# Three edits to the order of work at a seam: end transposes behind three of four contraction tiles, one split exchanged, and a group of transposes moved by one step

## The chip, the cores and the metric

The kernel runs on one core of one Trainium2 chip. The metric is the device time in microseconds (us) of one execution. Engines are named as the profile names them: PE is TensorE's matmuls, PEld its weight loads, DVE is VectorE, ACT is ScalarE, POOL is GpSimd, SP is SyncE.

## The reference

The model is a two-layer decoder trunk over 512 tokens of width 1024: a gated short-convolution layer with its feed-forward part, then a sliding-window attention layer (16 heads of 64, 4 key/value heads, window 128, a sink per head) with its feed-forward part. Cut to what lies on both sides of the seam:

```python
# end of layer 0
ff = swiglu(rmsnorm(h, ffn_pre_norm[0]), ffn_w_gate_up[0], ffn_w_down[0])
h = h + rmsnorm(ff, ffn_post_norm[0])
# start of layer 1
kv = rmsnorm(h, kv_norm) @ w_kv                 # shared keys and values
q = (rmsnorm(h, b_pre_norm[0]) @ b_w_q[0])      # queries
```

Both normed inputs of layer 1 have the same row factor and differ in the gain of each feature alone: one gain for keys and values (`kv_norm`), one for queries (`b_pre_norm`).

## The kernel before, in words

Everything is fp32, and products keep nearly fp32's accuracy with three matmuls in a short format: each operand is split into a rounded part `hi` (made by ACT) and a remainder `lo` (made by DVE, which reads `hi`), and `mm3` issues `whi*xlo`, `whi*xhi`, `wlo*xhi`.

The residual stream `h` lies as four tiles of 128 tokens by 1024 features (t = 0 to 3). What follows needs it with the features on the partitions, so the class `Update` does, for each token tile t: add the new contribution (`take`), sum its squares (`square_mix`), scale by the gain behind the norm (`scale`), work out the row factor (`mean`, DVE, with a power on POOL), update `h` (`update`), sum the squares of the new `h` (`square`), the next row factor (`mean2`, DVE and POOL), and scale into `xn[t]` (`norm`, ACT). Then `turn(b, ts)` transposes on PE the feature tiles b and b+4 of the token tiles `ts` into one PSUM bank, and `split(n, f, hf)` reads a quarter of such a bank for feature tile f twice: ACT writes `hi` (L350), DVE writes `lo` (L351). n = 0 is the copy for keys and values, n = 1 that for queries. hf = 0 holds the tokens of t = 0 and 1, hf = 1 those of t = 2 and 3. So a bank b of one half is read by four splits, each by two engines: (0, b), (0, b+4), (1, b), (1, b+4). There are two banks in each of two pools for these tiles, so that bank b of half 1 is the bank b of half 0 over again.

The seam runs so:

- `close` (L869) ends the feed-forward part: eight units of PE work (token tile t, half of the output columns), each with `n` = 4 contraction tiles of three matmuls of 512 columns. In the last unit, t = 3, half 1, the transposes of the tokens 0 and 1 (16, four per bank) stand between contraction tiles, and behind the unit the four splits (0, 0..3) of half 0 are issued. `close` is called three times (L961, L1188, L1534); the second call is this seam.
- `last_tile` (L909) then holds the norm of the last two token tiles and, in the gaps, lists of splits of half 0, called `pieces`. `pieces[3]` stands ahead of `norm(3)`, `pieces[4]` behind it.
- The loop at L1431 makes keys and values on PE: for each half, for each feature tile k, 12 matmuls of 256 columns. In half 0, behind k = 6 and k = 7, stand the transposes of the tokens 2 and 3 (`turn(b, (2, 3))`) with the splits (0, b) of half 1. Half 1 of the loop reads those.

The whole runs in the program's own order on PE, DVE, ACT and POOL (`tc.manual_schedule(engines=ALL)`): each engine works through its instructions in the order in which these lines issue them, and the framework adds the waits. Loads go through SP's queue and sums of weight blocks in memory through POOL's.

Of the kernel before, what the change touches and what calls it, by code (L numbers as in the profile page):

```python
# [73 lines left out]
def yoco_kernel(  # L74
# [38 lines left out]
    def name(s):  # L113
        uid[0] += 1
        return f"{s}_{uid[0]}"
# [13 lines left out]
    def bank(s, pool=None):  # L129

        if pool is None:
            pool = (ps_mm, ps_sc, ps_mm, ps_pt)[turn[0] % 4]
            turn[0] += 1
        return pool.tile([P, S], F32, tag="bank", name=name(s))
# [39 lines left out]
    def split_weights(src, raw=None, slots=False):  # L174
        if raw is None:
            raw = fetch(src)
        if slots:
            hi, lo = Two("whi", F32R), Two("wlo", F32R)
            for h in range(2):
                c = slice(h * S, (h + 1) * S)  # L180
                nc.scalar.activation(hi[:, c], raw[:, c], AF.Copy)
                nc.vector.tensor_tensor(out=lo[:, c], in0=raw[:, c], in1=hi[:, c].bitcast(F32),
                                        op=ALU.subtract)
            return hi, lo
        hi = wsp.tile([P, D], F32R, tag="whi", name=name("whi"))
        lo = wsp.tile([P, D], F32R, tag="wlo", name=name("wlo"))
        nc.scalar.activation(hi, raw, AF.Copy)
        nc.vector.tensor_tensor(out=lo, in0=raw, in1=hi.bitcast(F32), op=ALU.subtract)
        return hi, lo
# [14 lines left out]
    def unit(ps, t, ws, x, ks, n, k0=0, c0=0, c1=S):  # L204

        tk = slice(t * P, (t + 1) * P)
        for k in ks:
            w = ws[k // 2]
            kk = slice((k % 2) * S + c0, (k % 2) * S + c1)
            mm3(ps, x[k0 + k][0][:, tk], x[k0 + k][1][:, tk], w[0][:, kk], w[1][:, kk],  # L210
                k == 0, k == n - 1)
# [344 lines left out]
    for l in range(2):  # L556
# [3 lines left out]
        for rd, (f0, f1) in enumerate(ROUNDS[:-1]):  # L560
            k = slice(f0 // 2, f1 // 2)
# [50 lines left out]
    def seven(acts, n, mix, first):  # L612
# [9 lines left out]
        def product(p, ks, hi, lo):  # L622
# [34 lines left out]
    ws = [[wsp.tile([P, D], F32R, tag=tag, name=name(tag)) for tag in ("whi", "wlo")]  # L657
          for _ in range(3)]
# [10 lines left out]
    with tc.manual_schedule(engines=ALL):  # L669
# [25 lines left out]
        for k in range(KT):  # L695
# [7 lines left out]
            for i in range(3):  # L703
                for t in range(3):
                    n = 3 * k + t
# [9 lines left out]
        ws = [split_weights(None, raw, True) for raw in later[:2]]  # L715
# [21 lines left out]
    ys, acts, mix_c = [], [], [None] * NB  # L737
    both = []
    res = Update(mix_c, B_CONV, [G_FPRE[0]])
# [83 lines left out]
    with tc.manual_schedule(engines=ALL):  # L823
# [29 lines left out]
        ws = [line[f"w{n}"].w for n in range(4)]  # L853
# [12 lines left out]
        if square:  # L866
            res.square(t)

    def close(ws, x, k0, res, ahead, then=None, each=2):  # L869


        n = len(x) - k0

        def part(ps, t, half, ks):
            unit(ps, t, ws[len(ws) // 2 * half :], x, ks, n, k0)

        begun = [bank("pmix", ps_mm) for _ in range(2)]
        for half in range(2):
            part(begun[half], 0, half, range(n - 1))
            for _ in range(each if half == 0 or each > 1 else 0):  # L880
                ahead.one()
        for t in range(NB):
            for half in range(2):
                if t == 0:
                    ps = begun[half]
                    part(ps, t, half, range(n - 1, n))
                else:
                    ps = bank("pmix", ps_mm)
                    if (t, half) == (NB - 1, 1):
                        part(ps, t, half, range(2))  # L890
                        for b in range(4):
                            res.turn(b, (0, 1))
                        part(ps, t, half, range(2, n))
                        for f in range(4):
                            res.split(0, f, 0)
                        res.square_mix(t, 0)
                        res.square(NB - 2)
                        res.scale(t, 0)
                    else:
                        part(ps, t, half, range(n))  # L900
                res.take(t, half, ps)
                if (t, half) != (NB - 1, 0):
                    res.square_mix(t, half)
            if t < NB - 1:
                tile_done(res, t, square=t < NB - 2)
            if t == 0 and then:
                then()

    def last_tile(res, pieces, ahead=None):  # L909


        def some(i):
            for n, *f in pieces[i]:
                if n == "keep":
                    res.keep(f[0], 0, f[1])
                elif n == "weights":
                    ahead.slots()
                else:
                    res.split(n, f[0], 0)

        res.mean2(2)
        res.norm(2)
        res.mean(3)
        res.scale(3, 1)
        some(0)
        res.update(3)
        some(1)
        res.square(3)
        some(2)
        res.mean2(3)  # L930
        some(3)
        res.norm(3)
        some(4)
# [14 lines left out]
    def first_weights(l):  # L948
        return ([w_gu[l, f, j] for f in range(2) for j in range(2)]
                + [w_gb[l, 0, b] for b in range(2)])  # L950
# [3 lines left out]
    ahead = Ahead(first_weights(0))  # L954
# [9 lines left out]
    def ffn(l, before, ahead, gain, gpres, following):  # L964
# [152 lines left out]
        acts = [[] for _ in ROUNDS]  # L1117
        mix = [None] * NB
        pss = [bank("pgu", ps_mm) for _ in range(4)]
        with tc.manual_schedule(engines=ALL):  # L1120
# [44 lines left out]
            n = f1 - f0  # L1165
# [12 lines left out]
        res = Update(mix, gain, gpres)  # L1178
# [5 lines left out]
        ws = [job.w for job in closing]  # L1184
        if gpres:
            ahead = Ahead(following)
            with tc.manual_schedule(engines=ALL):
                close(ws, acts[-1], 0, res, ahead)  # L1188
            return res, ahead
        with tc.manual_schedule(engines=ALL):  # L1190
            for t in range(NB):
                for half in range(2):
                    if (t, half) == (NB - 1, 1):
                        for c in (0, 256):
                            ps = bank("pmix")
# [5 lines left out]
                    else:  # L1201
                        ps = bank("pmix")
# [16 lines left out]
    res, ahead = ffn(0, res, ahead, B_FFN[0], [G_KV, G_BPRE], [  # L1219
        w_k[0], w_k[1], w_v[:, 0:D], w_v[:, D:], w_q[0], w_q[1]])  # L1220
# [205 lines left out]
    at = []  # L1426

    with tc.manual_schedule(engines=ALL):
        last_tile(res, [[(0, 4)], [(0, 5)], [], [(0, 6), (0, 7), (1, 0), (1, 1)],
                        [(1, f) for f in (4, 5, 2, 3, 6, 7)]])  # L1430
        for hf in range(2):  # L1431
            c = slice(hf * 256, (hf + 1) * 256)
            for k in range(KT):
                kk = slice(k * P, (k + 1) * P)
                for ps, (whi, wlo) in zip(pk, wk):
                    mm3(ps[:, c], whi[:, kk], wlo[:, kk], xkv[k][0][:, c], xkv[k][1][:, c],
                        k == 0, k == KT - 1)
                values(2 * hf, k)
                values(2 * hf + 1, k)
                if hf == 0 and k >= 6:  # L1440
                    for b in (2 * k - 12, 2 * k - 11):
                        res.turn(b, (2, 3))
                        res.split(0, b, 1)
            if hf == 0:
                for f in range(4, KT):
                    res.split(0, f, 1)
            if hf == 0:
                ahead.one()
                for f in range(KT):
                    res.split(1, f, 1)  # L1450
                ahead.one()
                qs[0].w, qs[1].w = ahead.ready[4:]


        vt = [halves("vt", F32R) for _ in range(NB)]
        for pair in vt:
            for v in pair:
                nc.gpsimd.memset(v.bitcast(F32), 0.0)

        last_p = [slot("lp", F32R) for i in range(2)]  # L1460
        for p in last_p:
            nc.gpsimd.memset(p.bitcast(F32), 0.0)
        for part in range(4):
            qs[0].project(part)
        ks = [rope_split(rope(pk[0], nc.vector), nc.vector)]
        qs[LEAD].weights()
        nc.scalar.activation(warm, ones[:, 0:1], AF.Exp)
        for part in range(4):
            qs[1].project(part)
        qs[0].rotate(nc.vector)  # L1470
        qs[0].split(nc.vector)
        dst = [[v.rearrange("p (h d) -> p h d", d=2 * HD)[:, :, :HD] for v in pair]
               for pair in vt]
        src = [p.rearrange("p (h d) -> p h d", d=HD) for p in pv]
        for j in range(NB):
            nc.scalar.activation(dst[j][0], src[j], AF.Copy)
        for j in range(NB):
            nc.vector.tensor_tensor(out=dst[j][1], in0=src[j], in1=dst[j][0].bitcast(F32),
                                    op=ALU.subtract)

    with tc.manual_schedule(engines=ALL):
        sum_on("a0")
        for i in range(KT + 2):
            if i == KT:
                res = Update(mix_o, B_ATT, [G_FPRE[1]])
                res.leaves = True
                ahead = Ahead(first_weights(1))
            if i == KT + 1:
                res.load()
            for c in ORDER.split():  # L1490
# [13 lines left out]
                op, n = c[0], [int(d) for d in c[1:].rstrip("-")]  # L1504
                t = i - late
# [19 lines left out]
                else:  # L1525
                    t = 2 * (t - EARLY - 1) + n.pop(0)
# [104 lines left out]
```

## Time and profile before

| | before |
|---|---|
| median of 3 runs | 1020.13 us (1019.88 to 1020.14) |
| profiled execution, its own time | 1020.08 us |
| its span | 1018.3 us |
| PE / PEld / DVE / ACT / POOL busy | 99% / 88% / 85% / 57% / 19% |
| mean granted clock of TensorE | 0.999 |
| the seam (first of the end transposes to the first matmul of half 1) | 508.83 to 525.99 us of the span |

A row of the timeline gives the start of a group of instructions in us of the span, the time from its first start to its last end, the engine, the line, the tiles written and read, how many there are, and in brackets the engine's idle time before them with what ended it. Matmuls overlap: what counts for PE is the distance from start to start. The row of a line's own view gives the shortest, median and longest duration in ns. The waits view gives the engine, what waited, what it waited for, and the sum, number and longest of the waits in us.

### The profile page before, as it was taken

Reading aid. Unit: us, or ns where it says so; the run is one execution under the profiler, and the core shown is the slowest. Engines: PE = TensorE matmul, PEld = TensorE weight load, DVE = VectorE, ACT = ScalarE, POOL = GpSimd, SP = SyncE. Lnnn points to the kernel's source line nnn. Section 1 sums busy time; section 2 is a strip of 40 time slices with the busy share of each in tenths; the row PEclk is TensorE's granted clock in tenths of the full one; section 3 lists DMA queues with packets and bytes.
Section 4 is the critical chain, followed back from the end, with each engine's and each line's share of the span. In section 5 each row is a group of like instructions: output and inputs, shape, how many; then the busy total and the mean of one; then the engine's idle time right before and its main releaser. Section 6 shows DMA issues by size and latency. Waiting matters only on the chain.

```text
span 1018.3 us, 16274 instructions
## 1 busy us (share of the span) xinstructions
PE 1009.6 (99%) x6008; PEld 892.7 (88%) x6008; DVE 867.5 (85%) x1480; ACT 581.2 (57%) x1035; POOL 194.6 (19%) x259
## 2 busy tenths in 40 slices
PE   9999999999999999999999999999999999999997
PEld 8888888999889898998898888889998998989986
DVE  5766767899789999998869998778997899999896
ACT  6322444875655555566566776677666564645641
POOL 0443033102101011000122653221111010110001
PEclk9999999999999999999999999999999999999999
DMA  9997789549979699779504889976899576979742
GB/s 355 288 269 220 183 257 344 158 166 279 343 239 297 216 298 334 234 219 324 183 2 141 205 243 273 246 278 151 270 291 330 169 245 233 284 273 273 245 164 83
DMA packets 66575, 244.50 MB, mean 240 GB/s; under 512 B 7872, under 2 KB 8384, under 8 KB 54720
## 3 DMA queue, kind: packets, MB, share of 16 engines
q1 hardware_dynamic: 51328, 145.98, 38.8%
q0 software_dynamic: 14592, 96.48, 37.5%
q8 instruction: 47, 0.77, 0.3%
q10 hardware_dynamic: 576, 1.02, 0.3%
q14 instruction: 32, 0.26, 0.1%
HBM read 237.15 MB, written 102.76 MB: 334 GB/s over the span
## 4 chain that ended last, share of the span: by engine, by line
PE 93%; DVE 3%; ACT 2%; issue 1%; DMA 0%; POOL 0%; DVEq 0%; SPq 0%; ACTq 0%
PE gx L1055 14%; PE gx L1058 7%; PE pcub L194 4%; PE pcub L192 4%; PE pcub L193 4%; PE gz L194 4%; PE gz L193 4%; PE gz L192 4%; PE px L192 3%; PE px L193 3%; PE px L194 3%; PE pmix L193 2%; PE pmix L192 2%; PE pmix L194 2%; PE gy L194 2%; PE gy L193 2%
## 5 line engine op out<-in xcount | busy, mean ns | idle before, releaser
L478 DVE TENSOR_TENSOR wlo<-raw,whi 128x1024 fp32r<-128x1024 f32 x225 | 274.6, 1225 | 53.1 <-ACT whi L477 53.0
L477 ACT ACTIVATE whi<-raw 128x1024 fp32r<-128x1024 f32 x225 | 233.6, 1050 | 102.3 <-DVE raw L465 28.7
L1055 PE MATMUL gx<-xt,whi 128*128 128x512 f32 x480 | 120.4, 393 | 0.0
L1055 PEld LDWEIGHTS gx<-xt,whi 128*128 128x128 f32 x480 | 86.3, 189 | 15.5
L546 POOL DMA_DIRECT2D hsum<-in_w_gb_dram x96 | 62.8, 735 | 151.0 <-ACT whi L477 90.2
L546 POOL DMA_DIRECT2D hsum<-hsum x32 | 25.2, 789 | 294.3 <-ACT whi L477 219.3
L1017 DVE TENSOR_TENSOR st<-gx,st 128x256 f32<-128x256 f32 x200 | 77.9, 419 | 2.6 <-ACT st L1033 0.5
L1033 ACT ACTIVATE st<-gx 128x256 f32<-128x256 f32 x120 | 43.2, 380 | 62.6 <-PE gx L1058 58.9
L1058 PEld LDWEIGHTS gx<-xt,wlo 128*128 128x128 f32 x480 | 65.5, 190 | 4.7
L1058 PE MATMUL gx<-xt,wlo 128*128 128x256 f32 x480 | 66.9, 282 | 0.0
L1069 ACT ACTIVATE gr<-gr 128x1024 f32<-128x1024 f32 x20 | 21.3, 1063 | 50.1 <-DVE gr L1017 50.1
L192 PE MATMUL px<-wlo,ahi 128*128 128x512 f32 x120 | 46.8, 390 | 0.1
L194 PE MATMUL px<-whi,alo 128*128 128x512 f32 x120 | 46.7, 389 | 0.0
L193 PE MATMUL px<-whi,ahi 128*128 128x512 f32 x120 | 46.7, 389 | 0.0
L194 PE MATMUL gz<-xhi,wlo 128*128 128x256 f32 x160 | 45.5, 284 | 0.0
L193 PE MATMUL gz<-xt,whi 128*128 128x256 f32 x160 | 45.3, 283 | 0.0
L192 PE MATMUL gz<-xt,whi 128*128 128x256 f32 x160 | 45.3, 283 | 0.0
L193 PE MATMUL gy<-xhi,whi 128*128 128x256 f32 x160 | 45.3, 283 | 0.0
L192 PE MATMUL gy<-xlo,whi 128*128 128x256 f32 x160 | 45.3, 283 | 0.0
L194 PE MATMUL gy<-xhi,wlo 128*128 128x256 f32 x160 | 45.3, 283 | 0.0
L192 PE MATMUL gz<-xlo,whi 128*128 128x256 f32 x160 | 45.3, 283 | 0.0
L194 PE MATMUL gz<-xt,wlo 128*128 128x256 f32 x160 | 45.3, 283 | 0.0
(298 smaller groups left out, 2991.7 us busy)
## 6 DMA issues: line engine op xcount, KB each, us to landing
hsum<-in_w_gb_dram POOLq DMA_DIRECT2D x96, 512.0 KB, 7.9
raw<-hsum SPq DMA_DIRECT2D x88, 512.0 KB, 8.1
raw<-in_w_gb_dram SPq DMA_DIRECT2D x60, 512.0 KB, 7.1
hsum<-in_w_dn_dram POOLq DMA_DIRECT2D x36, 512.0 KB, 8.4
raw<-in_w_dn_dram SPq DMA_DIRECT2D x32, 512.0 KB, 6.3
hsum<-hsum POOLq DMA_DIRECT2D x28, 512.0 KB, 5.6
raw<-in_w_in_dram SPq DMA_DIRECT2D x21, 512.0 KB, 7.8
hsum<-in_w_dn_dram POOLq DMA_DIRECT2D x12, 768.0 KB, 13.1
```

What stands on the lines that cost most here:

```text
L192: nc.tensor.matmul(out, whi, xlo, start=start, stop=False, **kw)
L193: nc.tensor.matmul(out, whi, xhi, start=False, stop=False, **kw)
L194: nc.tensor.matmul(out, wlo, xhi, start=False, stop=stop, **kw)
L477: self.begun = nc.scalar.activation(hi[:, :n], raw, AF.Copy)
L478: nc.vector.tensor_tensor(out=lo[:, :n], in0=raw, in1=hi[:, :n].bitcast(F32), op=ALU.subtract)
L546: nc.gpsimd.dma_start(dst, src, max_dma_last_dim=4 * 4 * S, **kw))
L1017: nc.vector.tensor_tensor(out=out, in0=a, in1=b, op=ALU.add)
L1033: nc.scalar.activation(ste, a, AF.Copy)
L1055: nc.tensor.matmul(banks[c][e], whi[:, kk], factors[p][k][2], start=opened and k == 0, stop=False, **kw)
L1058: nc.tensor.matmul(banks[c][e][:, :256], wlo[:, kk], factors[p][k][0], start=False, stop=k == 3 and p == 4, **kw)
L1069: nc.scalar.activation(kept[2], kept[2], AF.Silu)
```

## The change

In the second call of `close` the end transposes stand behind three of the four contraction tiles in place of two. In `pieces`, the queries' splits (1, 1) and (1, 4) change places, and the rest of the list behind `norm(3)` goes from 4, 5, 2, 3, 6, 7 to 1, 5, 2, 6, 3, 7. In half 0 of the loop, behind k = 6 only bank 0 is transposed and its split issued, and behind k = 7 banks 1, 2 and 3, in place of two and two.

```diff
-    def close(ws, x, k0, res, ahead, then=None, each=2):
+    def close(ws, x, k0, res, ahead, then=None, each=2, lead=2):
...
                     if (t, half) == (NB - 1, 1):
-                        part(ps, t, half, range(2))
+                        part(ps, t, half, range(lead))
                         for b in range(4):
                             res.turn(b, (0, 1))
-                        part(ps, t, half, range(2, n))
+                        part(ps, t, half, range(lead, n))
...
-                close(ws, acts[-1], 0, res, ahead)
+                close(ws, acts[-1], 0, res, ahead, lead=3)
...
-        last_tile(res, [[(0, 4)], [(0, 5)], [], [(0, 6), (0, 7), (1, 0), (1, 1)],
-                        [(1, f) for f in (4, 5, 2, 3, 6, 7)]])
+        last_tile(res, [[(0, 4)], [(0, 5)], [], [(0, 6), (0, 7), (1, 0), (1, 4)],
+                        [(1, f) for f in (1, 5, 2, 6, 3, 7)]])
...
                 if hf == 0 and k >= 6:
-                    for b in (2 * k - 12, 2 * k - 11):
+                    for b in ((0,), (1, 2, 3))[k - 6]:
                         res.turn(b, (2, 3))
                         res.split(0, b, 1)
```

## The prediction

> **What bounds the kernel now.** I read the page first, then PE's waits, then the timeline of the seam engine by engine. The page and PE's waits:
>
> ```profile
> span 1018.3 us, 16274 instructions
> PE 1009.6 (99%) x6008; PEld 892.7 (88%) x6008; DVE 867.5 (85%) x1480; ACT 581.2 (57%) x1035; POOL 194.6 (19%) x259
> PE 93%; DVE 3%; ACT 2%; issue 1%; DMA 0%; POOL 0%; DVEq 0%; SPq 0%; ACTq 0%
> PE idle L675 <- DVE ones L141: 1.1, 1, 1.1
> PE xt L337 <- DVE xlo L351: 0.2, 1, 0.2
> PE xt L337 <- ACT xn L326: 0.2, 1, 0.2
> ```
>
> PE sets the time. After the start it waits visibly only twice, both times in L337, the transposes of this seam. What the change adds to or takes from PE's order there passes to the end almost undiminished. PE at the seam:
>
> ```profile
> 508.60 0.39 PE L194 MATMUL pmix<-whi,alo 128*128 128x512 f32 x1
> 508.83 0.27 PE L337 MATMUL xt<-ident,xn 128*128 128x128 f32 x1
> 509.32 1.86 PE L337 MATMUL xt<-ident,xn 128*128 128x128 f32 x15 [0.21 <-ACT xn L326]
> 510.93 0.48 PE L192 MATMUL pmix<-wlo,ahi 128*128 128x512 f32 x1
> 512.39 0.28 PE L192 MATMUL pk<-xhl,whi 128*128 128x256 f32 x1
> ...
> 522.34 0.28 PE L194 MATMUL pv<-whi,xlo 128*128 128x256 f32 x1
> 522.86 1.07 PE L337 MATMUL xt<-ident,xn 128*128 128x128 f32 x8 [0.24 <-DVE xlo L351]
> 523.68 0.36 PE L192 MATMUL pk<-xlo,whi 128*128 128x256 f32 x1
> 525.20 1.04 PE L337 MATMUL xt<-ident,xn 128*128 128x128 f32 x8
> 525.99 0.36 PE L192 MATMUL pk<-xhl,whi 128*128 128x256 f32 x1
> ```
>
> Two holes, start to start: 508.83 to 509.32 (0.49, where transposes otherwise follow at 0.11: 15 in 509.32 to 510.93) and 522.34 to 522.86 (0.52, where 0.12 is usual). So at most 0.38 + 0.40 = 0.78 us can be won. Now ACT and DVE at the same place; L350 is a split's `hi`, L351 its `lo`, L326 the norm:
>
> ```profile
> 508.13 1.13 ACT L326 ACTIVATE xn<-h,ur 128x1024 f32<-128x1024 f32 x1
> 509.90 1.79 ACT L350 ACTIVATE xhl<-xt,gt 128x256 fp32r<-128x256 f32 x4 [0.64 <-PE xt L337]
> 519.25 1.55 ACT L350 ACTIVATE xhi<-xt,gt 128x256 fp32r<-128x256 f32 x4
> 520.67 1.16 ACT L326 ACTIVATE xn<-h,ur 128x1024 f32<-128x1024 f32 x1
> 521.71 1.58 ACT L350 ACTIVATE xhi<-xt,gt 128x256 fp32r<-128x256 f32 x4
> 523.53 0.87 ACT L350 ACTIVATE xhi<-xt,gt 128x256 fp32r<-128x256 f32 x2 [0.24 <-DVE xlo L351]
> 534.76 1.65 ACT L350 ACTIVATE xhi<-xt,gt 128x256 fp32r<-128x256 f32 x4 [0.22 <-DVE xlo L351]
> 511.31 1.65 DVE L351 SCALAR_TENSOR_TENSOR xhl<-xt,gt,xhl 128x256 fp32r<-128x256 f32 x4
> 519.73 1.66 DVE L351 SCALAR_TENSOR_TENSOR xlo<-xt,gt,xhi 128x256 fp32r<-128x256 f32 x4 [0.21 <-ACT xhi L350]
> 520.52 0.48 DVE L351 SCALAR_TENSOR_TENSOR xlo<-xt,gt,xhi 128x256 fp32r<-128x256 f32 x1
> 522.23 1.66 DVE L351 SCALAR_TENSOR_TENSOR xlo<-xt,gt,xhi 128x256 fp32r<-128x256 f32 x4 [0.84 <-ACT xhi L350]
> 523.02 0.87 DVE L351 SCALAR_TENSOR_TENSOR xlo<-xt,gt,xhi 128x256 fp32r<-128x256 f32 x2
> 524.04 0.88 DVE L351 SCALAR_TENSOR_TENSOR xlo<-xt,gt,xhi 128x256 fp32r<-128x256 f32 x2 [0.15 <-ACT xhi L350]
> 534.25 3.22 DVE L351 SCALAR_TENSOR_TENSOR xlo<-xt,gt,xhi 128x256 fp32r<-128x256 f32 x8
> 519.60 0.54 POOL L321 TENSOR_TENSOR ur<-uv,mhalf 128x1 f32<-128x1 f32 x1 [3.38 <-DVE uv L317]
> ```
>
> The two rows where a `hi` waits for a `lo` decide the forecast, for `hi` needs no `lo` as data. At 523.53 stands hi(1,6): it begins when lo(1,2), first of the pair at 523.02, ends at 523.50. At 534.76 stands the fifth of eight splits (1, f) of half 1, hi(1,4); it begins when lo(1,0), first at 534.25, has run its 0.48 (534.73). Each time the two share a bank (2 and 6; 0 and 4), and the four `hi` before them, on four different banks, go 0.36 apart without a wait ((1.58 - 0.47) / 3). So ACT does not read a bank until DVE's earlier read of that bank has ended. A split followed by one on the same bank therefore costs the full hi-lo-hi round.
>
> The Trainium skill, page "PSUM — Partial Sum Buffer", section "PSUM bank collisions raise a hardware error", says that two engines must be kept from one bank at once, reads against reads included, and that schedulers add a dependency between them. By that rule the exchange of splits must wait as below; without it the sum would be that of the first rival. The two rows agree with it.
>
> **The change part by part.** No edit adds or removes an instruction; `turn` and `split` issue PE, ACT and DVE work alone, so SP's and POOL's queues are passed by nothing.
>
> *End transposes one contraction tile later.* Three matmuls (0.23 apart: 508.60 to 508.83) go ahead, so transposes begin at 508.83 + 0.68 = 509.51. The second of them needs xn[1], ready at 508.13 + 1.13 = 509.26: no wait. Sixteen at 0.11 end at 511.18, the last three matmuls bring pk to about 511.96, against 512.39: 0.4 won on PE. Price: the first `hi` goes from 509.90 to 510.15. Cover: lo(0,0) starts at 511.31 behind other DVE work, and hi(0,0) ends at 510.15 + 0.47. DVE keeps its times, so the norms behind it do too. First pk needs lo(0,0) at 511.78: met by 0.2. Were that cover gone, up to 0.25 would come back.
>
> *(1,4) ahead of norm(3).* ACT begins its group of four at 519.25; the third, hi(1,0), keeps its time, and lo(1,0) runs 520.52 to 521.00. The fourth was hi(1,1) on another bank, at 520.31; now it is hi(1,4) on bank 0 and begins at 521.00 + 0.03 = 521.03 (hand-off: 523.50 to 523.53). Queued behind it on ACT is norm(3), whose row factor POOL has had since 520.14: it goes from 520.67 to 521.39 and ends at 522.55, not 521.83. Waiting for that is the transpose of token tile 3. PE, 0.43 earlier, is through k = 6 at 522.03; bank 0 is free at lo(1,4)'s end, 522.02 + 0.15 (522.71 to 522.86, the first `lo` of the group at 522.23) = 522.17, but tile 3 comes at 522.55 + 0.05 (as 509.26 to 509.32) = 522.61. Four transposes, then k = 7 begins at 522.91 and takes 525.20 - 523.68 = 1.52, to 524.43. Before, eight transposes had been done by 523.68 and k = 7 by 525.20.
>
> *The six splits behind norm(3), now 1, 5, 2, 6, 3, 7.* Neighbours share a bank. norm(3) began 1.04 before the next `hi` (520.67, 521.71), so hi(1,1) starts at 522.43. Durations:
>
> ```profile
> L350 ACT ACTIVATE xhi<-xt,gt x40: 453/476/517, 182.3 to 693.8; 128x256 fp32r<-128x256 f32 x40
> L351 DVE SCALAR_TENSOR_TENSOR xlo<-xt,gt,xhi x40: 473/477/487, 182.8 to 694.5; 128x256 fp32r<-128x256 f32 x40
> ```
>
> I take 0.475 and 0.477, 0.033 from `hi`'s end to `lo` (521.71 + 0.49 to 522.23) and back, and 0.40 from one `lo` to the next on DVE ((1.66 - 0.48) / 3). lo(1,1) 522.94 to 523.42; hi(1,5) 523.45; lo(1,5) 523.96 to 524.44, freeing bank 1. hi(1,2) follows on ACT at once, but lo(1,2) stands behind lo(1,5): 524.36 to 524.84. hi(1,6) 524.87, lo(1,6) 525.38 to 525.86, freeing bank 2. lo(1,3) 525.78 to 526.25, hi(1,7) 526.29, lo(1,7) 526.80 to 527.27, freeing bank 3. Before, all six were through at 524.92 (524.04 + 0.88): the group lasts 4.84 from its first `hi` in place of 3.21, and starts 0.72 later.
>
> *Three banks behind k = 7.* Queued on PE behind these transposes is all of half 1. PE comes at 524.43; bank 1 takes writes at 524.44 + 0.15 = 524.59 (waits 0.16), bank 2 at 526.01 where PE would be there at 525.03 (waits 0.98), bank 3 at 527.42 where PE would be there at 526.45 (waits 0.97). Four transposes cost 0.39 (eight: 525.20 to 525.99). Half 1 then begins at 527.81 against 525.99. Its own first need, lo(0,0) of half 1, follows lo(1,7) on DVE at 527.19 to 527.67, in time. Next late behind it would be the split (0,3) of half 1, needed three feature tiles (4.3 us) later: covered.
>
> *Sum.* Won: 0.43 and the old hole of 0.40. Lost: 0.14 before the first transpose of bank 0, 0.33 before its second (522.17 to 522.61, less 0.11), 0.16 + 0.98 + 0.97, and 0.07 because three more groups of transposes start from rest: 2.65. Net 527.81 - 525.99 = **+1.8 us**. What PE wins ahead of this counts for nothing: the end is set by ACT and DVE handing bank 3 over. In half 1 and the attention, loads and splits keep their distance to PE, which has no wait there to give it back. Of later waits this is the largest:
>
> ```profile
> PEld px L192 <- DVE wlo L478: 0.5, 1, 0.5
> ```
>
> If it hung on DVE work not itself driven by PE, up to 0.5 would return; I take 0, since DVE there follows PE's results. The profiled execution took 1020.08, 1.78 over its span and 0.05 under the median; so 1020.08 + 1.82 = 1021.90, as a median 1021.95 us. That is 0.18% slower. The least that a measurement of this kernel can tell from no change is about 0.2%, or 2.04 us (1022.17): the forecast, slower, lies just inside it.
>
> **The rivals.**
>
> *The new neighbours do not wait* (the change does what its order suggests). Then hi(1,4) starts at 520.31, norm(3) ends at 521.83, lo(1,4) at 521.39, and bank 0 is written without a hole at 522.03; k = 7 begins at 522.45, and the six `lo`, 0.39 apart from 522.23, free banks 1, 2, 3 at 523.11, 523.89 and 524.68, each as PE gets there (523.97, 524.40, 524.83). Half 1 begins at 525.23: -0.76, 1019.37 us. Against it stand the two rows at 523.53 and 534.76; for it, that only these two show the wait. Chance 0.12.
>
> *Slower by more than 0.2%: a hand-off costs more.* Four times a `hi` waits for the `lo` just before it in the series that sets the end ((1,4), (1,5), (1,6), (1,7)). I took 0.03 from the rows at 523.53 and 534.76; the dearest hand-off from DVE in these rows is 0.15, to PE at 522.86. At that price four cost 0.48 more: +2.3, 1022.4. It decides from 0.03 + 0.22 / 4, about 0.09, each. Chance 0.18.
>
> *The clock falls.* The granted clock at the end of the kernel, behind the last matmul:
>
> ```profile
> 1010.00:1014.00 4.00, 1.51 (x13) 1.31 (x11) 3.66 (x10) 0.70 (x4) 0.93 (x1) 1.00 0.33 133
> 1014.00:1016.00 2.00, 0.00 (x0) 0.00 (x0) 1.03 (x2) 0.00 (x0) 0.00 (x0) 0.99 0.36 138
> 1016.00:1018.30 2.30, 0.00 (x0) 0.00 (x0) 0.00 (x0) 0.00 (x0) 0.00 (x0) 0.50 0.28 108
> ```
>
> PE's 1.51 us of work end about 1011.5, and the clock halves only at about 1016. The new holes are under 1 us each, with transposes between; but from 524.43 to 527.81, 3.4 us, PE does nothing else than 12 transposes. If these did not count as work, the clock could halve, and as long a stretch again at half speed costs 1.7 us: +3.5, 1023.65 us. The Trainium skill, page "TensorE: Matmul & The Clock Gate", says that an idle window of about 3.4 us halves the clock (section "What's actually happening") and that transposes do not count as busy in the same way (section "Part 4: PE-mode transpose"); this case's trace agrees with the former, with some 4.4 us before the drop, and shows nothing on the latter. Chance 0.05.
>
> **How the numbers follow.** The forecast has 0.63: of this I put 0.13 over the bound of 2.04 (one hand-off or a late start of half 1 mis-sized by 0.2) and 0.50 within. For a large part given back later I put 0.02. Faster by over 0.2% would take 2.04 us where the holes hold 0.78: 0.02, taken out of the first rival's 0.12. Within 0.2%: 0.50 + 0.10 + 0.02 = 0.62. Slower by over 0.2%: 0.13 + 0.18 + 0.05 = 0.36. The range holds the forecast and the dearer hand-offs: from 0.5 given back (1021.4) to 0.2 over the second rival (1022.6). The first rival and the clock, 0.17, stay outside.
>
> **What would show it.** Right: no idle before L337 at 509.5; ACT idle for 0.6 before 521.03, put down to `lo` L351; norm(3) at 521.4; three waits of ACT L350 for DVE L351 of some 0.5 behind it; PE's waits in L337 at 522.6, 524.6, 526.0 and 527.4, the last two near 1 us; half 1 at 527.8; everything behind shifted by 1.8. Wrong: L350 rows of six in 2.2 us without idle (first rival); idle of over 0.1 between `lo`'s end and the next `hi` (second); matmuls of half 1 at 0.24 in place of 0.12 with a granted clock under 1.00 (third); a lead at 526 that is lost by 690.

## The result, and the profile after

| | before | after |
|---|---|---|
| median, 22 runs each | 1020.13 us | 1022.21 us |
| lowest to highest | 1019.78 to 1022.34 | 1021.56 to 1026.15 |
| profiled execution, its span | 1018.3 us | 1020.4 us |

After to before the ratio is 1.0022, 95% interval 1.0016 to 1.0028: 2.08 us slower, just past the bound of 2.04 us (0.2%) and inside the stated range. Seven of the 22 runs after show a mean granted clock of 0.997 and take 1023.18 us or more (an eighth, at 1023.31, shows 0.999); the median of the 14 others is 1021.9. The clock as the cause of the seven is taken up below.

PE's waits after, in the waits view (engine, what waited, for what, us in total, times, longest):

```profile
PE xt L337 <- DVE xlo L351: 1.6, 2, 0.8
PE idle L675 <- DVE ones L141: 1.1, 1, 1.1
PE pcub L707 <- ACT whi L678: 0.5, 1, 0.5
```

The wait for the norm (`xn`) among the end transposes is gone; that for `lo` (L351), once 0.2, is now two of 0.8. The last row is the kernel's start. PE's timeline after:

```profile
509.67 1.91 PE L337 MATMUL xt<-ident,xn 128*128 128x128 f32 x16
511.33 0.48 PE L192 MATMUL pmix<-wlo,ahi 128*128 128x512 f32 x1
512.11 0.28 PE L192 MATMUL pk<-xhl,whi 128*128 128x256 f32 x1
...
522.06 0.28 PE L194 MATMUL pv<-whi,xlo 128*128 128x256 f32 x1
522.34 0.97 PE L337 MATMUL xt<-ident,xn 128*128 128x128 f32 x4
523.07 0.36 PE L192 MATMUL pk<-xlo,whi 128*128 128x256 f32 x1
524.77 0.63 PE L337 MATMUL xt<-ident,xn 128*128 128x128 f32 x4
526.19 0.63 PE L337 MATMUL xt<-ident,xn 128*128 128x128 f32 x4 [0.79 <-DVE xlo L351]
527.61 0.63 PE L337 MATMUL xt<-ident,xn 128*128 128x128 f32 x4 [0.80 <-DVE xlo L351]
527.99 0.36 PE L192 MATMUL pk<-xhl,whi 128*128 128x256 f32 x1
```

The 16 end transposes run without a hole. Behind k = 7 (523.07 to 524.77) come three groups of four, 1.42 apart, though four transposes take only about 0.4. The view's 0.8 counts from the modelled end of the transpose before; from start to start, as the prediction counts, each of the last two groups is 1.42 - 0.44 = 0.98 late. ACT and DVE after show why:

```profile
508.28 1.14 ACT L326 ACTIVATE xn<-h,ur 128x1024 f32<-128x1024 f32 x1
519.41 1.19 ACT L350 ACTIVATE xhi<-xt,gt 128x256 fp32r<-128x256 f32 x3
521.20 0.47 ACT L350 ACTIVATE xhi<-xt,gt 128x256 fp32r<-128x256 f32 x1 [0.60 <-DVE xlo L351]
521.57 1.14 ACT L326 ACTIVATE xn<-h,ur 128x1024 f32<-128x1024 f32 x1
522.61 0.46 ACT L350 ACTIVATE xhi<-xt,gt 128x256 fp32r<-128x256 f32 x1
523.63 0.84 ACT L350 ACTIVATE xhi<-xt,gt 128x256 fp32r<-128x256 f32 x2 [0.56 <-DVE xlo L351]
525.05 0.84 ACT L350 ACTIVATE xhi<-xt,gt 128x256 fp32r<-128x256 f32 x2 [0.58 <-DVE xlo L351]
526.47 0.48 ACT L350 ACTIVATE xhi<-xt,gt 128x256 fp32r<-128x256 f32 x1 [0.58 <-DVE xlo L351]
524.14 0.88 DVE L351 SCALAR_TENSOR_TENSOR xlo<-xt,gt,xhi 128x256 fp32r<-128x256 f32 x2 [0.55 <-ACT xhi L350]
525.56 0.88 DVE L351 SCALAR_TENSOR_TENSOR xlo<-xt,gt,xhi 128x256 fp32r<-128x256 f32 x2 [0.54 <-ACT xhi L350]
526.98 0.48 DVE L351 SCALAR_TENSOR_TENSOR xlo<-xt,gt,xhi 128x256 fp32r<-128x256 f32 x1 [0.54 <-ACT xhi L350]
```

Each of the four splits that follow one on their own bank, (1,4), (1,5), (1,6) and (1,7), has its `hi` waiting 0.56 to 0.60 for the `lo` before it, and the `lo` waits again for that `hi`. A bank costs a round of 1.42 (523.63, 525.05, 526.47).

Traces differ ahead of the seam, by some tenths and once by over 2 us, so I measure the seam from the start of the norm that the end transposes need (the first row above) to the start of half 1: 525.99 - 508.13 = 17.86 us before, 527.99 - 508.28 = 19.71 after, +1.85. All seams below are given so, against 17.86.

### The profile page after: what moved, and what is told of

It reads as the page before. It is cut to its first block, busy times and chain, and to the rows that moved or that the text cites. A ratio compares the mean times of both kernels' runs of the same rounds, so it can differ in the third digit from the quotient of the medians.

```text
span 1020.4 us, 16274 instructions
## 1 busy us (share of the span) xinstructions
PE 1010.0 (99%) x6008; PEld 892.4 (87%) x6008; DVE 868.0 (85%) x1480; ACT 582.0 (57%) x1035; POOL 195.0 (19%) x259
## 4 chain that ended last, share of the span: by engine, by line
PE 92%; DVE 4%; ACT 2%; issue 1%; DMA 0%; POOL 0%; DVEq 0%; SPq 0%; ACTq 0%
PE gx L1055 14%; PE gx L1058 7%; PE pcub L192 4%; PE pcub L194 4%; PE pcub L193 4%; PE gz L194 4%; PE gz L192 4%; PE gz L193 4%; PE px L192 3%; PE px L193 3%; PE px L194 3%; PE pmix L192 2%; PE pmix L193 2%; PE pmix L194 2%; PE gy L194 2%; PE gy L193 2%
```

## The experiments

The theory: ACT reads a bank only when DVE's earlier read of it has ended; neighbours on one bank make a series of hi-lo-hi rounds, and the series' end, not PE's own order, sets the start of half 1. The rival: PE's new order (three groups behind k = 7) or the late norm makes the loss. Each of these banks is one tile of the program, so no run tells whether the wait goes by bank or by tile. For the runs at a clock of 0.997 there is a theory of its own, the clock. "Tail" is the list of splits behind `norm(3)`; "holes" are PE's waits ahead of banks 2 and 3 in the kernel after. Each ratio is to executions of the kernel before made beside the run.

| kernel | median, us | ratio to before, 95% interval | seam against 17.86 |
|---|---|---|---|
| end transposes alone | 1020.24 | 1.0000 (0.9991 to 1.0008) | 0.00 |
| lists of splits alone | 1021.82 | 1.0017 (1.0008 to 1.0026) | +1.83 |
| later transposes alone | 1020.49 | 1.0003 (0.9995 to 1.0012) | +0.01 |
| the change, tail 1, 2, 3, 5, 6, 7 | 1019.98 | 0.9999 (0.9990 to 1.0008) | +0.02 |
| the change once more | 1021.91 | 1.0023 (1.0013 to 1.0033) | +2.06 (profiled with a fallen clock) |
| holes filled with matmuls | 1021.82 | 1.0019 (1.0010 to 1.0028) | +1.84 |
| holes filled with transposes | 1022.15 | 1.0021 (1.0011 to 1.0030) | +1.83 |
| no neighbours on one bank | 1019.37 | 0.9996 (0.9987 to 1.0005) | -0.86 |
| the same once more | 1019.16 | 0.9989 (0.9980 to 0.9998) | -0.86 |
| the same, end transposes as before | 1019.52 | 0.9994 (0.9985 to 1.0003) | -0.42 |
| the same, later transposes as before | 1019.58 | 0.9994 (0.9985 to 1.0003) | -0.44 |

**The end transposes alone.** Only `lead=3` in the second call of `close`; lists and later transposes as before.

> The first edit alone: the end transposes behind three contraction tiles, both lists of splits and the later transposes as before. Bank theory (ScalarE reads a bank only when VectorE's earlier read of it has ended, and the series of splits sets when bank 0 is free): the first hole closes, PE reaches k = 6's end 0.4 us earlier and waits that much longer for lo(1,4), whose time does not move (522.7): half 1 begins where it did, 0.0 us, and the run takes what the kernel before takes. Rival (PE's order alone sets the time): 0.4 us faster.

The first hole closed and the second grew by as much:

```profile
PE idle L675 <- DVE ones L141: 1.1, 1, 1.1
PE xt L337 <- DVE xlo L351: 0.7, 1, 0.7
```

One wait of 0.7 in place of two of 0.2; the seam is the same to 0.01 us (525.69 - 507.83). By itself the first edit is worth nothing, as the theory says.

**The lists alone.**

```diff
-        last_tile(res, [[(0, 4)], [(0, 5)], [], [(0, 6), (0, 7), (1, 0), (1, 1)],
-                        [(1, f) for f in (4, 5, 2, 3, 6, 7)]])
+        last_tile(res, [[(0, 4)], [(0, 5)], [], [(0, 6), (0, 7), (1, 0), (1, 4)],
+                        [(1, f) for f in (1, 5, 2, 6, 3, 7)]])
```

> The second edit alone: (1,4) ahead of norm(3) and the rest as 1, 5, 2, 6, 3, 7; the transposes where they were before, two banks behind k = 6 and two behind k = 7. Bank theory: the series of splits ends as in the changed kernel (bank 3 free at 527.4), so half 1 begins at 527.8: +1.8 us, nearly all of the loss of the whole change; PE's largest hole is now ahead of bank 1, behind k = 6 (about 1.6 us). Rival (the loss comes from the transposes moved behind k = 7): 0 to 0.3 us slower.

The whole loss is here (527.88 - 508.19 = 19.69, +1.83), though PE's order is that of before. PE's timeline:

```profile
522.52 0.69 PE L337 MATMUL xt<-ident,xn 128*128 128x128 f32 x4
524.66 0.63 PE L337 MATMUL xt<-ident,xn 128*128 128x128 f32 x4 [1.45 <-DVE xlo L351]
526.56 0.60 PE L337 MATMUL xt<-ident,xn 128*128 128x128 f32 x4
527.49 0.63 PE L337 MATMUL xt<-ident,xn 128*128 128x128 f32 x4 [0.33 <-DVE xlo L351]
```

The waits stand elsewhere (1.45 ahead of bank 1, 0.33 ahead of bank 3), the end is the same: bank 3 is handed over when the series is through. The rival is refuted for the order of PE.

**The later transposes alone.** Only `for b in ((0,), (1, 2, 3))[k - 6]`.

> The third edit alone: one bank behind k = 6 and three behind k = 7, both lists as before. Bank theory: bank 0 is written at 522.86 as before, k = 7 runs 523.3 to 524.8, banks 1, 2, 3 are free at 523.3, 524.7 and 525.1, so half 1 begins at 526.05: +0.05 us, not to be told from 0. Rival (the loss comes from the transposes moved behind k = 7): +1.5 us or more.

Seam +0.01. The median is 0.3 us up, inside its interval; three groups behind k = 7 cost nothing by themselves.

**The change with another tail.**

```diff
-                        [(1, f) for f in (1, 5, 2, 6, 3, 7)]])
+                        [(1, f) for f in (1, 2, 3, 5, 6, 7)]])
```

> The changed kernel with one line different: the six splits behind norm(3) in the order 1, 2, 3, 5, 6, 7, so that neighbours have different banks, (1,4) still next to (1,0) ahead of norm(3). Bank theory: norm(3) is as late as in the changed kernel (521.4 on the clock of the kernel before), but the six hi go 0.36 apart, their lo 0.39 apart, bank 3 is free at 525.5 and half 1 begins at about 525.9: -0.1 us against the kernel before, 1.9 us faster than the changed kernel. Rival (the late norm(3) or the moved transposes make the loss): +1 us or more against the kernel before. Clock theory for the runs of the changed kernel that lie 1.4 us over the others at a granted clock of 0.997 (the clock falls in the hole of two waits of 1 us): with the holes gone, none of those here beyond what the kernel before shows.

ACT's timeline of this kernel:

```profile
521.07 0.47 ACT L350 ACTIVATE xhi<-xt,gt 128x256 fp32r<-128x256 f32 x1 [0.61 <-DVE xlo L351]
521.44 1.14 ACT L326 ACTIVATE xn<-h,ur 128x1024 f32<-128x1024 f32 x1
522.48 2.28 ACT L350 ACTIVATE xhi<-xt,gt 128x256 fp32r<-128x256 f32 x6
```

(1,4) still waits 0.61 behind (1,0), and norm(3) is as late as after; but the six `hi` take 2.28 in one piece, and 1.83 us of the seam are back. So the late norm is not the loss, the order of the tail is. The seam is 526.04 - 508.16 = 17.88, +0.02 where -0.1 was forecast: that sum looked at bank 3 alone, and PE waits 0.18 ahead of bank 1, whose last split, (1,5), now comes fourth. Same instructions, same banks, only other neighbours.

**The change once more, and its holes filled.** These three are about the runs at a granted clock of 0.997.

> The changed kernel once more. Of its 22 runs 14 lie at 1021.6 to 1022.7 us and 8 at 1023.2 us or more, 7 of these 8 with a mean granted clock of 0.997 in place of 0.998 to 0.999. Clock theory (in the stretch of 3.4 us with three waits and 12 transposes the clock falls to a half for one stretch, in the runs in which its steps happen to lie so): again about a third of the runs some 1.4 us above the rest, at 0.997, and where such a run is profiled, a granted clock of 0.5 for about 3.4 us behind the holes at 526 to 532. Rival (scatter of loads, as the kernel before has now and then): one run in ten at most.

Two of nine runs showed 0.997 (1023.14 and 1023.38 us), and the first of them was the profiled one; a third, at 1023.05, showed 0.998. The profiled run's windows (us busy and number for PE, PEld, DVE, ACT, POOL, then the granted clock):

```profile
524.00:527.30 3.30, 1.70 (x13) 1.10 (x12) 2.22 (x6) 2.14 (x7) 0.53 (x2) 1.00 0.00 0
527.30:530.70 3.40, 3.40 (x18) 3.40 (x18) 2.92 (x8) 2.21 (x6) 0.00 (x0) 0.50 0.00 0
530.70:534.10 3.40, 3.40 (x30) 3.40 (x30) 0.00 (x1) 0.00 (x0) 0.00 (x0) 1.00 0.00 0
```

The granted clock is 0.50 from 527.3 to 530.7, right behind the holes, and full again after that. The holes alone do not bring it about: in the first profiled execution of the changed kernel the same stretch and the one behind it (0.4 us later in its span) look alike, and the clock stays full:

```profile
524.40:527.80 3.40, 1.79 (x13) 1.20 (x13) 2.31 (x7) 2.24 (x7) 0.59 (x2) 1.00 0.00 0
527.80:531.20 3.40, 3.40 (x31) 3.40 (x30) 2.89 (x8) 2.18 (x6) 0.00 (x0) 1.00 0.00 0
```

PE's timeline of the run whose clock fell:

```profile
528.55 0.41 PE L192 MATMUL pk<-xhl,whi 128*128 128x256 f32 x1
528.76 0.41 PE L193 MATMUL pk<-xhl,whi 128*128 128x256 f32 x1
528.97 0.41 PE L194 MATMUL pk<-xhl,wlo 128*128 128x256 f32 x1
...
530.94 0.28 PE L192 MATMUL pk<-xhl,whi 128*128 128x256 f32 x1
531.06 0.28 PE L193 MATMUL pk<-xhl,whi 128*128 128x256 f32 x1
531.18 0.28 PE L194 MATMUL pk<-xhl,wlo 128*128 128x256 f32 x1
```

Matmuls 0.21 apart, then 0.12. The first matmul of the queries before, after and in this run:

```profile
537.58 0.40 PE L192 MATMUL pq<-xlo,whi 128*128 128x512 f32 x1
539.59 0.40 PE L192 MATMUL pq<-xlo,whi 128*128 128x512 f32 x1
540.64 0.40 PE L192 MATMUL pq<-xlo,whi 128*128 128x512 f32 x1
```

From the same norm as above (508.13, 508.28 and 507.84) that is 29.45, 31.31 and 32.80: this run is 3.35 us behind before, the other profiled run 1.86. So the fallen clock costs 1.5 us.

The two fillers, ahead of the transposes of banks 1 and 2, one of matmuls and one of transposes:

```diff
                     for b in ((0,), (1, 2, 3))[k - 6]:
+                        if b in (1, 2):
+                            res.banks[b, 1] = bank("xt", (ps_pt, ps_sc)[b % 2])
+                            for i in range(4):
+                                w = wk[i % 2][0][:, :P]
+                                nc.tensor.matmul(res.banks[b, 1], w, wv[0][0][:, :S], start=True, stop=True)
                         res.turn(b, (2, 3))
```

> The changed kernel with four matmuls of 512 columns into the bank just freed, ahead of the transposes of bank 1 and of bank 2, which overwrite them (4 x 0.23 = 0.9 us each): the holes are filled with PE work that nothing uses. Bank theory: bank 3 is free at the same time, so the lower cluster of times stays where the changed kernel has it, within 0.1 us of 1021.8. Clock theory: the upper cluster (1023.2 and above, clock 0.997) is gone. Rival (scatter of loads): the same share of runs in the upper cluster as in the changed kernel beside it.

```diff
-                        res.turn(b, (2, 3))
+                        for _ in range(3 if b in (1, 2) else 1):
+                            res.turn(b, (2, 3))
```

> The changed kernel with the transposes of bank 1 and of bank 2 made three times over (8 more of 0.11 us = 0.9 us each, the same values): the holes are filled with transposes in place of matmuls. Lower cluster as in the changed kernel, about 1021.8. If transposes count as work for the clock: no upper cluster. If they do not: the upper cluster of the changed kernel (about a third of the runs at 1023.2 and above, clock 0.997) stays.

Both leave the seam where the change put it (+1.84 and +1.83 us) although PE has hardly a hole in it, which again shows that PE's work is not what sets the end. With transposes (half 1 at 528.28, the norm at 508.59) they go in one piece:

```profile
525.07 3.46 PE L337 MATMUL xt<-ident,xn 128*128 128x128 f32 x28
```

At a clock of 0.997 were none of 11 and none of 10 runs, against 9 of 31 of the change as it is (7 of 22 and 2 of 9). Taken together, 0 of 21 against 9 of 31 speaks for the holes as what lets the clock fall; beside the fillers alone it was 2 of 9, too few by themselves. None of the other versions in the table, 88 runs, nor any of the 89 runs of the kernel before beside them that count in its ratios, showed 0.997. Only one fallen clock was traced; the other eight are told by the mean. For transposes alone, 0 of 10 is thin, but does not show them to count for less than matmuls. The matmul filler had one run at 1023.89 with a clock of 0.999, which the clock does not explain.

**No neighbours on one bank.** The three edits' places, with the lists respaced:

```diff
-        last_tile(res, [[(0, 4)], [(0, 5)], [], [(0, 6), (0, 7), (1, 0), (1, 4)],
-                        [(1, f) for f in (1, 5, 2, 6, 3, 7)]])
+        last_tile(res, [[(0, 4)], [(0, 5), (1, 0)], [], [(0, 6), (0, 7), (1, 4), (1, 1)],
+                        [(1, f) for f in (5, 2, 3, 6, 7)]])
```

> The changed kernel with the queries' splits so placed that no two neighbours on ScalarE share a bank: (1,0) next to (0,5), where ScalarE waits for VectorE anyway, then (0,6), (0,7), (1,4), (1,1) ahead of norm(3) and 5, 2, 3, 6, 7 behind it. Bank theory: norm(3) is back at 520.7, lo(1,4) ends at 521.0, banks 1, 2, 3 are free at 522.9, 524.3 and 524.7 as PE gets there, both holes of the kernel before are closed and half 1 begins at 525.2: -0.75 us against the kernel before (1019.3 to 1019.4), -2.6 us against the changed one. Rival (the norms, not the banks, set the end, or what is won is given back behind the seam): 0.0 +- 0.2 against the kernel before. Clock theory: no upper cluster.

> The kernel with no two neighbours on one bank (all three edits' places, the lists respaced) once more, to narrow its interval. Bank theory: 1019.3 to 1019.4 us as the first time, 0.65 to 0.75 us under the kernel before. Rival (the first median was scatter): within 0.3 us of the kernel before.

Medians 1019.37 and 1019.16. The first interval reaches over 1, the second does not: 0.9989 (0.9980 to 0.9998). Both seams are 17.00 (527.44 - 510.44 and 525.00 - 508.00). The first's profiled execution took 1021.52 us at a clock of 0.999: PE waits 1.3 us for DVE (L647) at 290 us, far ahead of the seam. Such scatter, without the clock, stands in these medians too. The second kernel's PE and ACT:

```profile
521.89 0.60 PE L337 MATMUL xt<-ident,xn 128*128 128x128 f32 x4
523.76 1.47 PE L337 MATMUL xt<-ident,xn 128*128 128x128 f32 x12
516.80 0.48 ACT L350 ACTIVATE xhi<-xt,gt 128x256 fp32r<-128x256 f32 x1 [0.19 <-DVE xlo L351]
519.11 1.55 ACT L350 ACTIVATE xhi<-xt,gt 128x256 fp32r<-128x256 f32 x4
520.53 1.16 ACT L326 ACTIVATE xn<-h,ur 128x1024 f32<-128x1024 f32 x1
521.58 1.21 ACT L350 ACTIVATE xhi<-xt,gt 128x256 fp32r<-128x256 f32 x3
523.00 0.86 ACT L350 ACTIVATE xhi<-xt,gt 128x256 fp32r<-128x256 f32 x2 [0.21 <-DVE xlo L351]
```

No transpose of the seam waits. hi(1,0) at 516.80 still waits 0.19, in a gap in which ACT had nothing else to do; the pair at 523.00 waits 0.21 and is not late for PE. The seam is 0.86 us shorter than before and 2.71 shorter than after. This version beats both.

**The respaced lists with one edit taken back.** Each has one line of the kernel above as it was before: the call of `close` without `lead=3`, and the later transposes two and two.

> The respaced lists and the later transposes as in the kernel above, but the end transposes behind two contraction tiles as before (the first hole of 0.4 us is open again). Bank theory: with the series of splits out of the way PE's order sets the time, so the first edit, worth 0.0 by itself, is worth 0.4 here: about 0.35 us under the kernel before, 0.4 over the kernel above. Rival (the first edit is worth nothing anywhere): equal to the kernel above.

> The respaced lists and the end transposes behind three tiles, but the later transposes two and two as before. Bank theory: bank 1 is wanted at 522.5 on the clock of the kernel before and free at 522.9, so a hole of 0.35 us opens ahead of k = 7: about 0.4 us under the kernel before, 0.35 over the kernel with all three. Rival (the third edit is worth nothing anywhere): equal to it.

Seams -0.42 (525.66 - 508.22) and -0.44 (525.17 - 507.75) against -0.86: with the series out of the way the end transposes are worth 0.44 us and the later transposes 0.42. The respaced lists without either edit were not run. The medians (1019.52 and 1019.58 against 1019.16) say the same, but their intervals overlap, so it rests on the traces.

## Why the prediction was right

**Bound.** Right: from the seam on, what PE loses stays lost. The seam cost 1.85 us; from the same norm to the start of the kernel's last matmul it is 1013.29 - 508.28 against 1011.23 - 508.13, 1.91.

**End transposes.** Right: 0.4 was forecast and 0.43 came: after, the first matmul of the keys comes 512.11 - 508.28 = 3.83 behind the norm, before 512.39 - 508.13 = 4.26. And that this counts for nothing was shown by that edit alone.

**(1,4) next to (1,0).** Right: `hi` 0.60 late, norm(3) at 521.57 - 0.15 = 521.42 (after, the norm ahead of the seam starts 0.15 later) where 521.39 stood.

**The tail.** Right: the groups of transposes begin, less 0.15, at 524.62, 526.04 and 527.46 where 524.59, 526.01 and 527.42 stood, half 1 at 527.84 where 527.81 stood. The waits ahead of bank 0's second transpose and of bank 1, forecast as 0.33 and 0.16, are too small for the waits view and show in the starts alone: at 522.34 four transposes take 0.97 where 0.63 stands at 524.77, and the last matmul ahead of 524.77 starts 0.30 before it where 0.12 is usual. One small slip in the working changes nothing: (1.58 - 0.47) / 3 is 0.37, not 0.36.

**First rival** (the neighbours do not wait): refuted by the waits of 0.56 to 0.60. Its -0.76 for half 1 is near the -0.86 of the kernel without such neighbours. That the first median of that kernel is the rival's 1019.37 to the digit is luck: the second is 1019.16.

**Second rival** (a dearer hand-off): refuted. After, DVE's pair at 524.14 ends at 525.02 and the next `hi` starts at 525.05; the pair at 525.56 ends at 526.44, the next `hi` starts at 526.47: 0.03, as taken.

**Third rival** (the clock falls): this is the step that was mis-sized, in its chance and not in its price. I gave it 0.05 as a thing that happens or not; it happens in some executions of the same program, 9 of 31 by the mean clock. The price, 1.7 foretold, was 1.5. Without the seven runs at 0.997 the median after is 1021.91, next to the forecast's 1021.95; with them it is 1022.21. So the forecast, just inside the bound of 2.04 us, had the seam right, and a rival that it had left outside its range carried the median just past that bound. The Trainium skill, "TensorE: Matmul & The Clock Gate", section "What's actually happening", asks for an idle window. The stretch ahead of the drop shows PE busy for 1.70 of 3.30 us, almost all of it with transposes, so whether the trace differs from that depends on whether these count as busy; 0 of 10 with the holes full of transposes speaks for it and does not settle it.

## What to carry to other kernels

In these traces two engines that read one PSUM bank take turns, so in an order written by hand put work on different banks between two pairs that share one; here the same instructions in another order were 2.7 us apart. When a series on other engines sets when PE may go on, moving PE's own work is worth nothing until that series is shortened, and then each move is worth what it promised (0.0 alone, over 0.4 with the lists respaced). A hole in PE can cost more than its length: behind these the clock fell in 9 of 31 runs, for 1.5 us in the one that was traced.

## What the runs showed of the hardware that was not expected

In one trace the granted clock halved for 3.4 us behind a stretch in which PE was busy for 1.70 of 3.30 us and never without a start for as much as 1.1 us. The mean clock of 0.997 that goes with it stood in 9 of 31 executions of one program, in none of the 21 in which the same holes were filled, and not in the lists alone (11 runs), whose holes of 1.45 and 0.33 us lie further apart. Where the line runs between these, no run here settles.
